# Two-layer hybrid encoder: FFN tiles placed anew, inputs normalised by halves, residual spilled by half rows

## The chip, the cores and the metric

One NeuronCore of one Trainium2 chip runs the whole program. The metric is the device time of one execution in microseconds. The kernel before took 2791.24 us as the median of three runs (2791.16, 2791.24 and 2794.4).

The engines are called PE (matrix products), DVE (VectorE), ACT (ScalarE), POOL (GpSimd) and SP (SyncE, which only issues DMAs here). Each works through its own queue in order. The queues' order is not the program's: a planner in the compiler puts each engine's instructions in order beforehand, by times that it estimates itself.

## What is computed

Two encoder layers on 1024 tokens of width 1024, all in float32. Layer 0 mixes tokens with differential attention, layer 1 with windowed grouped-query attention. Each layer then has a gated FFN with a depthwise convolution over positions, and a gated projection of a second input `p`:

```python
for i in range(DEPTH):                       # DEPTH = 2
    hn = rms_norm(h, attn_norm[i])
    mix = diff_attention(hn, ...) if i == 0 else windowed_gqa(hn, ...)
    h = h + mix                              # mix ends in a product with w_o
    h = h + conv_ffn(rms_norm(h, ffn_norm[i]), ffn_w_up[i], ffn_conv_w[i], ffn_conv_b[i], ffn_w_down[i])
    gate = sigmoid(rms_norm(h, ple_norm[i]) @ ple_w_gate[i])
    h = h + (p[i] @ ple_w_proj[i]) * gate
return rms_norm(h, final_norm)

def conv_ffn(h, w_up, conv_w, conv_b, w_down):        # D_FF = 2816
    u = h @ w_up                                      # 1024 x 5632
    u = sum(pad(u)[:, t:t + S] * conv_w[t] for t in range(3)) + conv_b
    gate, val = split(u, 2)
    return (silu(gate) * val) @ w_down
```

## The kernel before, in words

Activations lie transposed: features on the 128 partitions, the 1024 positions along the free dimension, in two halves of 512 (`HS`, index `hf`). `res[kt]`, kt = 0 to 7, is the residual stream. To keep float32 precision with fast products, each operand is split into a high part (a cast on ACT, L132 `copy_hi`) and the rest (a subtraction on DVE or POOL, L138 `sub_lo`), and each product is made of three matmuls (L227 to L229 in `mm3`, L1084 to L1086 in `product`).

Per layer the stages follow one another: projection to q, k, v; attention; `projected` (L1378), which holds the out-projection `out_proj` (L936), `p_proj` (L1243), `seven_inputs` (L988) and `ffn_up` (L1088); then `ffn_down` (L1179) and the gated projection. Each stage takes its tiles from pools that are stacked upon each other in on-chip memory. When a stage ends its pools go, and the next stage's pools are stacked from the same base. A tile of the new stage waits until the old tiles that lay at its place are done with, tile by tile. Within one pool the tags lie in the order in which they are first used.

- `out_proj` makes units of one row block and one half, 24 matmuls each. A unit's sum is taken off PSUM by an addition of the old residual (L964), which a DMA has fetched from the spill (L962). `half_order` (L970) has the last blocks run half 0, then half 1, and calls `done(hf)`, which gives `rstd[hf]`, the scale of the norm, by `norm_half` (L482). Afterwards the new residual is spilled whole (`spill_res`, L556), since its place is needed.
- `p_proj` makes `p @ ple_w_proj` in 16 units of 6 matmuls and stores them (L1277, L1279).
- `seven_inputs` normalises all of `res` (L1004, into tiles `nh`) and forms from it the inputs of the up-projection. The up-projection runs by a scheme of seven products for a 2 x 2 block product: 22 blocks j, each with seven products m1 to m7 of 12 matmuls. The inputs are b11 (`q1`), b21 and b22 (`qb`), t1 and t2 (`qa`, in the memory of the residual) and t3 and t4 (`qu`), each in two parts. `seven_weights` (L1039) makes the sums of the weights (`sf`, on DVE for the first two blocks, on POOL for the others) and splits four tiles of them (L1057, L1058); three of the four stand in the ring of `wh`/`wl` tiles, two of each, which `out_proj` and `p_proj` use as well.
- Block 0 runs the seven products side by side, k by k (L1121 to L1138), so that it can begin with the first inputs. The others run them one after another (L1139 to L1157). m1 and m2 add up in bank `pa`, m5 and m3 in bank `pc`; between m5 and m3, DVE reads m5 (L1149). The convolution follows (L1159 to L1177), and the result goes to memory as `gs[j]`.
- `ffn_down` takes two `gs` tiles a group (`load`, L1188: DMA into `gr`, high part `gh`, rest `gl`), 11 groups of 96 matmuls in 16 units. In group 0 the sum of a unit is added to the old residual, which comes by DMA from the spill (L1212 to L1214); in the others to `res` (L1216).

`stage` (L1373) makes the pools of the first projection, of `projected`'s first part, and of everything from `ffn_down` to the projection of layer 1. Its small pool (`t`, `n`) lies at the base, then come 24 places of 4 KB, of which the lists at L91 to L97 (`S_LOW`, `S_MID`, `S_END`, `XO`) give out numbers. Eight of these, `S_END`, hold a half of the normalised input in the projections, and `gh` and `gl` in `ffn_down`.

## Time and profile before

| | us |
|---|---|
| median of 3 runs | 2791.24 |
| the profiled execution, whole | 2790.52 |
| its span, first to last instruction | 2788.7 |
| PE busy | 2644.0 |
| DVE busy | 1958.8 |
| ACT busy | 1210.2 |
| POOL busy | 1016.0 |

The rows further down come from the profiled execution; times in them count from the span's start. A row of a timeline gives start and duration, engine, source line, operation, what it writes and reads, and in brackets how long its engine had been idle before it and what ended that. A busy PE is not always a PE at its peak: matmuls overlap, and the clock that is granted to TensorE varies, so the windows give the mean granted clock (PEclk, 1.00 is 2.4 GHz, 0.50 is 1.2 GHz).

### The profile page before, as it was taken

What the parts mean: (1) busy time and instruction counts of PE and PEld (TensorE: products, weight loads), DVE (VectorE), ACT (ScalarE), POOL (GpSimd) and SP (SyncE); (2) the same over time, 40 slices, a digit from 0 to 9 for tenths busy, and PEclk for the clock granted to TensorE, in tenths of its full rate; (3) what the DMA queues carried; (4) which work ended last, traced back from release to release, by engine and by line L of the source; (5) the groups of instructions that cost most, each with busy time, mean ns of one, the idle gap of its engine ahead of it and who ended that gap; (6) DMA issues with size and microseconds to landing.
All of it is one profiled execution on the core that took longest, in us unless ns stands there. A gap on an engine that the chain in (4) does not pass through costs nothing. (4 is left out here: it accounts for less than half of the span.)

```text
span 2788.7 us, 33239 instructions
## 1 busy us (share of the span) xinstructions
PE 2644.0 (95%) x12606; PEld 2183.4 (78%) x12606; DVE 1958.8 (70%) x2314; ACT 1210.2 (43%) x2101; POOL 1016.0 (36%) x587
## 2 busy tenths in 40 slices
PE   8999899999899999979999999999799999799998
PEld 6888778878668888858888788887588888688877
DVE  7541588883498888856677756963798888666664
ACT  5322567772444444421136426963443444311152
POOL 2642577773013443422221354441034344222201
PEclk9999999999999999989999999999899999899999
DMA  6444423303322322253213346113222232443112
GB/s 225 167 152 150 136 61 107 106 5 106 132 64 81 91 72 87 91 175 112 91 46 127 135 162 227 46 61 130 82 87 72 91 91 68 157 132 104 61 61 98
DMA packets 201828, 296.23 MB, mean 106 GB/s; under 512 B 9268, under 2 KB 138437, under 8 KB 197957
## 3 DMA queue, kind: packets, MB, share of 16 engines
q1 hardware_dynamic: 201045, 293.72, 32.1%
q8 instruction: 99, 1.62, 0.3%
q14 instruction: 60, 0.49, 0.1%
q10 hardware_dynamic: 624, 0.39, 0.0%
HBM read 207.83 MB, written 86.25 MB: 105 GB/s over the span
## 5 line engine op out<-in xcount | busy, mean ns | idle before, releaser
L138 POOL TENSOR_TENSOR wl<-wr,wh 128x1024 fp32r<-128x1024 f32 (+1 forms) x113 | 293.1, 2609 | 817.6 <-ACT wh L132 743.9
L1048 POOL TENSOR_TENSOR sf<-wr 128x1024 f32<-128x1024 f32 x40 | 128.4, 3210 | 585.3 <-DVE w L1058 585.3
L1216 DVE TENSOR_TENSOR res<-res,ps 128x512 f32<-128x512 f32 x320 | 216.6, 684 | 140.4 <-PE ps L229 140.4
L227 PE MATMUL ps<-gh,wh 128*128 128x512 f32 x704 | 275.6, 397 | 34.9 <-ACT gh L132 32.3
L228 PE MATMUL ps<-gl,wh 128*128 128x512 f32 x704 | 275.5, 391 | 0.0
L229 PE MATMUL ps<-gh,wl 128*128 128x512 f32 x704 | 274.9, 391 | 0.0
L227 PE MATMUL ps<-hn,wh 128*128 128x512 f32 x544 | 214.7, 396 | 5.6 <-ACT wh L132 4.9
L228 PE MATMUL ps<-hn,wh 128*128 128x512 f32 x544 | 212.9, 392 | 0.0
L229 PE MATMUL ps<-hn,wl 128*128 128x512 f32 x544 | 212.4, 392 | 0.1
L132 ACT CAST wh<-wr 128x1024 fp32r<-128x1024 f32 (+1 forms) x140 | 144.9, 1091 | 121.5 <-PE ps L228 62.7
L132 ACT CAST gh<-gr 128x1024 fp32r<-128x1024 f32 x44 | 46.2, 1050 | 343.3 <-PE ps L229 328.9
L733 DVE TENSOR_REDUCE sm<-S 128x1 f32<-128x1024 f32 x128 | 152.0, 1215 | 56.0 <-PE S L732 54.9
L227 PEld LDWEIGHTS ps<-gh,wh 128*128 128x128 f32 x704 | 134.4, 191 | 66.3 <-ACT gh L132 34.1
L737 ACT ACTIVATE e<-S,sm 128x1024 f32<-128x1024 f32 x128 | 142.2, 1113 | 90.0 <-DVE sm L733 87.6
L1057 ACT CAST w<-sf 128x1024 fp32r<-128x1024 f32 x88 | 92.6, 1052 | 174.4 <-PE ps L1086 106.6
L228 PEld LDWEIGHTS ps<-gl,wh 128*128 128x128 f32 x704 | 133.3, 189 | 27.6
L229 PEld LDWEIGHTS ps<-gh,wl 128*128 128x128 f32 x704 | 133.0, 189 | 27.9
L749 POOL TENSOR_TENSOR e<-e,e 128x1024 f32<-128x1024 f32 x64 | 152.3, 2380 | 5.2
L1084 PE MATMUL ps<-qa,w 128*128 128x512 f32 x352 | 138.6, 397 | 10.5 <-ACT qa L1023 8.1
L1084 PE MATMUL ps<-qb,w 128*128 128x512 f32 x352 | 140.2, 398 | 6.0 <-DVE uv L1149 3.3
L1086 PE MATMUL ps<-qa,w 128*128 128x512 f32 x352 | 138.9, 395 | 2.6 <-DVE w L1058 2.6
L1085 PE MATMUL ps<-qa,w 128*128 128x512 f32 x352 | 139.3, 396 | 0.0
(259 smaller groups left out, 7210.3 us busy)
## 6 DMA issues: line engine op xcount, KB each, us to landing
wr<-ffn_w_up SPq DMA_DIRECT2D x88, 512.0 KB, 5.2
gs<-c SPq DMA_DIRECT2D x44, 512.0 KB, 2.9
wr<-ffn_w_down SPq DMA_DIRECT2D x22, 1024.0 KB, 5.0
gr<-gs SPq DMA_DIRECT2D x44, 512.0 KB, 3.7
spill<-res SPq DMA_DIRECT2D x32, 512.0 KB, 2.9
qs<-rhl SPq DMA_DIRECT2D x32, 512.0 KB, 3.1
old<-spill SPq DMA_DIRECT2D x64, 256.0 KB, 2.8
wr<-diff_w_qkv SPq DMA_DIRECT2D x12, 1024.0 KB, 5.9
```

The costliest lines, as they stand in the source:

```text
L132: self.nc.scalar.copy(out, in_)
L138: eng.tensor_tensor(out, in_, f32(hi), op=ALU.subtract)
L227: self.nc.tensor.matmul(out, ah, bh, start=first, stop=False)
L228: self.nc.tensor.matmul(out, ah, bl, start=False, stop=False)
L229: self.nc.tensor.matmul(out, al, bh, start=False, stop=last)
L733: v.tensor_reduce(sm[:, a : a + 1], ps[:], axis=AX.X, op=ALU.max, negate=True)
L737: nc.scalar.activation(e[:], ps[:], AF.Exp, bias=sm[:, a : a + 1], accum_out=sm[:, 2 + a : 3 + a])
L749: nc.gpsimd.tensor_tensor(ea[:], ea[:], eb[:], op=ALU.add)
L1084: mm(ps, ah, bh, start=first and i == 0, stop=False, skip_group_check=True)
L1085: mm(ps, ah, bl, start=False, stop=False, skip_group_check=True)
L1086: mm(ps, al, bh, start=False, stop=last and i == n - 1, skip_group_check=True)
L1216: v.tensor_tensor(self.res[dt][:, sl], self.res[dt][:, sl], acc[:], op=ALU.add)
```

## The change

- The residual's rows are paired (kt, kt + 4) in one tile instead of (2i, 2i + 1).
- `out_proj` spills each half row right after its addition, in 16 DMAs, to a new scratch tensor; `spill_res` is no longer called there. Its small pool has three `t` tiles instead of four.
- `seven_inputs` is split. `seven_begin` runs in `done(0)` and normalises half 0 of `res` in place, and makes b11 and b21. `seven_rest` runs after `p_proj` and makes the rest from half 1.
- The pools of both FFN stages are stacked anew. `qb` and `q1` lie at the base through all of `projected`; above them come first the tiles of `out_proj` (half 1, then half 0), later `qu`, `t`, `e`, `wd`, `sf`. `p_proj`'s output tiles are two of the places of half 0. In `stage` come `S_LOW` and four of `S_END`, then the small pool, then the other four of `S_END`, then `S_MID`, for all its users.
- The weight sums of block 1 are made on POOL.
- In the blocks after the first, m4 stands ahead of m5.
- In `ffn_down`, group 0 copies its sums into `res` on ACT; the old residual is added by POOL in groups 3 to 6, two whole rows in each.

```diff
     def rows_tile(self, rows, kt, name):
         if rows[kt] is None:
+            half = KT // 2
             t = self.resp.tile([P, 2, S], F32, tag="res", name=self.nm(name))
-            rows[kt // 2 * 2] = t[:, 0]
-            rows[kt // 2 * 2 + 1] = t[:, 1]
+            rows[kt % half] = t[:, 0]
+            rows[kt % half + half] = t[:, 1]
...
+        before = self.spill
+        self.spill = self.dram.tile([D, S], F32, name=self.nm("spill"))
...
-            nc.sync.dma_start(old, self.spill[dt * P : (dt + 1) * P, sl])
+            nc.sync.dma_start(old, before[dt * P : (dt + 1) * P, sl])
             self.rows_tile(self.res, dt, "res")
             nc.vector.tensor_tensor(self.res[dt][:, sl], pt[:], old, op=ALU.add)
+            nc.sync.dma_start(self.spill[dt * P : (dt + 1) * P, sl], self.res[dt][:, sl])
             self.norm_tile(st, dt, hf, self.res[dt][:, sl], t[:, 1])
-        self.half_order(w, blocks, unit, lambda hf: self.norm_half(st, hf, psum, END_BANKS))
+        def done(hf):
+            self.norm_half(st, hf, psum, END_BANKS)
+            if hf == 0:
+                self.seven_begin(layer, st["rstd"])
+
+        self.half_order(w, blocks, unit, done)
...
+    def normed(self, layer, kt, hf, rstd):
+        r = self.res[kt][:, hf * HS : (hf + 1) * HS]
+        self.nc.vector.scalar_tensor_tensor(
+            r, r, self.gcol("ffn", layer, kt), rstd[hf][:], op0=ALU.mult, op1=ALU.mult
+        )
+        return r
+
+    def two_parts(self, out, src, sign=None):
+        self.copy_hi(out[:, 0], src, sign)
+        self.sub_lo(self.nc.vector, out[:, 1], src, out[:, 0], sign)
+
+    def seven_begin(self, layer, rstd):
+        self.x7 = {n: [] for n in ("b11", "b21", "b22", "t1", "t2", "t3", "t4")}
+        for kp in range(KT // 2):
+            one = self.q1p.tile([P, 2, HS], F32R, "q1", self.nm("q1"))
+            self.two_parts(one, self.normed(layer, kp, 0, rstd))
+            self.x7["b11"].append((one[:, 0], one[:, 1]))
+            qb = self.qbp.tile([P, 2, 2, HS], F32R, "qb", self.nm("qb"))
+            self.two_parts(qb[:, :, 0], self.normed(layer, kp + KT // 2, 0, rstd))
+            for n, i in (("b21", 0), ("b22", 1)):
+                self.x7[n].append((qb[:, 0, i], qb[:, 1, i]))
+            self.x7["t1"].append(qb)
+
+    def seven_rest(self, layer, rstd, fp):
+        v = self.nc.vector
         sub = ALU.subtract
+        qbs, self.x7["t1"] = self.x7["t1"], []
         for kp in range(KT // 2):
+            n1 = self.res[kp]
+            n2 = self.res[kp + KT // 2]
+            b12 = self.normed(layer, kp, 1, rstd)
+            b22 = self.normed(layer, kp + KT // 2, 1, rstd)
             ta = fp.tile([P, 2, HS], F32, "t", self.nm("ta"))
             tb = fp.tile([P, 2, HS], F32, "t", self.nm("tb"))
+            v.tensor_tensor(ta[:, 0], b12, n1[:, :HS], op=sub)
+            v.tensor_tensor(ta[:, 1], b22, ta[:, 0], op=sub)
+            v.tensor_tensor(tb[:, 0], b12, b22, op=sub)
+            v.tensor_tensor(tb[:, 1], ta[:, 1], n2[:, :HS], op=sub)
+            self.two_parts(qbs[kp][:, :, 1], b22, -1.0)
             qa = self.resp.tile([P, 2, 2, HS], F32R, tag="res", name=self.nm("qa"))
             qu = fp.tile([P, 2, 2, HS], F32R, "qu", self.nm("qu"))
+            for q, t, names in ((qa, ta, ("t1", "t2")), (qu, tb, ("t3", "t4"))):
+                self.two_parts(q, t[:])
...
-            w = self.seven_weights(raw, fp, j < 2)
+            w = self.seven_weights(raw, fp, j < 1)
...
                 v.tensor_tensor(t3[:], t2[:], pd[:], op=ALU.add)
+                prod(pe, "m4")
+                v.tensor_tensor(uv[:, lo], t3[:], pe[:], op=ALU.subtract)
                 prod(pc, "m5")
                 v.tensor_tensor(uv[:, hi], t3[:], pc[:], op=ALU.add)
                 prod(pa, "m2", False)
                 nc.scalar.copy(ug[:, lo], pa[:])
-                prod(pe, "m4")
-                v.tensor_tensor(uv[:, lo], t3[:], pe[:], op=ALU.subtract)
                 prod(pc, "m3", False)
...
                 if g == 0:
                     self.rows_tile(self.res, dt, "res")
-                    old = tp.tile([P, HS], F32, tag="n", name=self.nm("old"))
-                    nc.sync.dma_start(old[:], self.spill[dt * P : (dt + 1) * P, sl])
-                    v.tensor_tensor(self.res[dt][:, sl], old[:], acc[:], op=ALU.add)
+                    nc.scalar.copy(self.res[dt][:, sl], acc[:])
...
+            if g in (3, 4, 5, 6):
+                for dt in (2 * g - 6, 2 * g - 5):
+                    old = tp.tile([P, S], F32, tag="t", name=self.nm("old"))
+                    nc.sync.dma_start(old[:], self.spill[dt * P : (dt + 1) * P, :])
+                    nc.gpsimd.tensor_tensor(self.res[dt], self.res[dt], old[:], op=ALU.add)
...
-    def stage(self, ctx, name, places=range(24)):
+    def stage(self, ctx, name):
+        hp = Bank(ctx, self.tc, f"h_{name}", S_LOW + [S_END[i] for i in (0, 4, 1, 5)])
         tp = self.slots(ctx, f"t_{name}", {"t": 4, "n": 2})
-        hp = Bank(ctx, self.tc, f"h_{name}", list(places))
+        rest = Bank(ctx, self.tc, f"i_{name}", [S_END[i] for i in (2, 6, 3, 7)] + S_MID)
+        hp.pools.update(rest.pools)
         return tp, hp
...
+        with ExitStack() as c0:
+            self.qbp = self.slots(c0, f"qb{layer}", {"qb": 4})
+            self.q1p = self.slots(c0, f"q1{layer}", {"q1": 4})
+            with ExitStack() as c:
+                hp = Bank(c, self.tc, f"h_w{layer}", XO[1] + XO[0])
+                tp = self.slots(c, f"t_w{layer}", {"t": 3, "n": 2})
+                psum = self.banks(c, f"w{layer}")
+                rstd = self.out_proj(w, hp, tp, psum, "ffn", layer)
+                for _ in self.p_proj(
+                    layer, out_pp, psum, BANKS,
+                    lambda n: hp.cycle(XO[0][5:7], [P, S], F32, n),
+                ):
+                    pass
+            with ExitStack() as c:
+                qu = self.slots(c, f"qu{layer}", {"qu": 4})
+                fp = self.slots(c, f"ft{layer}", {"t": 5})
+                fe = self.slots(c, f"fe{layer}", {"e": 4})
+                fw = self.slots(c, f"fw{layer}", {"wd": 2})
+                fs = self.slots(c, f"fs{layer}", {"sf": 1})
+                fp = Tags([qu, fp, fe, fw, fs])
+                psum = self.slots(c, f"pu{layer}", {"ps": 8}, PSUM)
+                x7 = self.seven_rest(layer, rstd, fp)
+                self.ffn_up(layer, x7, fp, psum, gs)
```

## Rows read from the trace of the kernel before

**Rows 1.** The page's busy line: us (share of the span) and instructions of each engine.

```profile
PE 2644.0 (95%) x12606; PEld 2183.4 (78%) x12606; DVE 1958.8 (70%) x2314; ACT 1210.2 (43%) x2101; POOL 1016.0 (36%) x587
```

**Rows 2.** Waits of PE: waiting line, releaser, us in total, times, longest.

```profile
PE ps L227 <- ACT gh L132: 32.3, 2, 16.2
PE ps L1084 <- ACT q L1011: 13.7, 5, 5.7
...
PE ps L1086 <- DVE w L1058: 2.6, 2, 1.3
```

**Rows 3.** Windows: length; busy PE, PEld, DVE, ACT, POOL; PEclk; DMA share; GB/s.

```profile
1217.86:1266.69 48.83, 46.85 (x192) 37.30 (x193) 28.52 (x37) 7.51 (x8) 4.77 (x2) 0.96 0.55 192
2431.15:2478.46 47.31, 46.92 (x192) 38.11 (x193) 27.76 (x37) 7.51 (x8) 5.75 (x2) 0.94 0.57 198
...
754.89:803.90 49.01, 37.86 (x113) 24.48 (x114) 48.29 (x66) 21.50 (x27) 0.00 (x0) 0.76 0.15 43
1017.70:1036.74 19.04, 19.04 (x85) 15.77 (x84) 16.67 (x15) 7.96 (x9) 7.82 (x4) 1.00 0.28 83
714.90:735.10 20.20, 19.01 (x88) 14.88 (x87) 9.99 (x14) 9.67 (x14) 5.18 (x2) 1.00 0.60 191
735.10:749.10 14.00, 14.00 (x63) 11.36 (x61) 0.00 (x0) 8.05 (x16) 0.00 (x0) 1.00 0.67 267
```

**Rows 4.** Timeline where `p_proj` ends: its last matmul on PE; DVE's next operation.

```profile
748.83 0.39 PE L229 MATMUL ps<-wh,wl 128*128 128x512 f32 x1
...
750.15 1.22 DVE L1058 TENSOR_TENSOR w<-wr,w 128x1024 fp32r<-128x1024 f32 x1 [15.13 <-ACT w L1057]
```

**Rows 5.** Groups by line, 750 to 803.9 (ACT: from 735): count, busy us, mean ns.

```profile
L1004 DVE SCALAR_TENSOR_TENSOR nh<-res,par,rstd 128x512 f32<-128x512 f32 x16 | 11.0, 742 | 2.1 <-DMA pp<-pp 2.1
...
L1024 DVE TENSOR_TENSOR qu<-tb,qu 128x1024 fp32r<-128x1024 f32 x4 | 4.9, 1215 | 0.0
...
L1015 DVE TENSOR_TENSOR ta<-nh 128x512 f32<-128x512 f32 x4 | 2.7, 680 | 0.0
...
L1277 ACT COPY pp<-ps 128x512 f32<-128x512 f32 x16 | 8.7, 602 | 7.5 <-PE ps L229 7.5
```

**Rows 6.** Timeline of PE at the end of `ffn_up` in layer 0.

```profile
1194.28 0.39 PE L1086 MATMUL ps<-qu,w 128*128 128x512 f32 x1
...
1198.58 0.50 PE L1084 MATMUL ps<-qb,w 128*128 128x512 f32 x1 [1.65 <-DVE uv L1149]
...
1217.86 1.65 PE L227 MATMUL ps<-gh,wh 128*128 128x512 f32 x3 [16.22 <-ACT gh L132]
```

**Rows 7.** SP's queue at the same place.

```profile
1208.45 0.37 SPq L159 DMA_DIRECT2D wr<-ffn_w_down  x1
1211.94 0.34 SPq L1177 DMA_DIRECT2D gs<-c  x1
1212.37 2.91 SPq L1190 DMA_DIRECT2D gr<-gs  x4
```

**Rows 8.** DMA issues: count, KB each, median us from issue to landing.

```profile
old<-spill SPq DMA_DIRECT2D x64, 256.0 KB, 2.8
```

**Rows 9.** Timeline of POOL and DVE; then a line's durations, min/median/max ns.

```profile
1017.18 3.33 POOL L1048 TENSOR_TENSOR sf<-wr 128x1024 f32<-128x1024 f32 x1 [11.07 <-DVE w L1058]
...
1018.28 3.30 DVE L1170 SCALAR_TENSOR_TENSOR c<-ug,conv,c 128x1023 f32<-128x1023 f32 x1
...
L1216 DVE TENSOR_TENSOR res<-res,ps x320: 667/686/689, 1250.1 to 2692.1; 128x512 f32<-128x512 f32 x160
```

**Rows 10.** Timelines of PE and SP at the attention's start; landing of a load.

```profile
251.50 0.39 PE L731 MATMUL S<-stk,stk 128*128 128x512 f32 x1
...
295.67 0.32 SPq L609 DMA_DIRECT2D stk<-ks  x1
...
311.72 0.55 PE L769 MATMUL ps<-v,aT 128*128 128x128 f32 x1 [1.79 <-DMA v<-vs]
...
stk<-ks SPq DMA_DIRECT2D x8, 1024.0 KB, 5.0
```

More of the change, by code (lines that the diff above doesn't have):

```diff
@@ L66, in tile, with __init__ @@
         return self.pool.tile(shape, dtype, tag=tag, bufs=self.bufs[tag], name=name)
+class Tags:
+    def __init__(self, slots):
+        self.of = {tag: s for s in slots for tag in s.bufs}
+    def tile(self, shape, dtype, tag, name):
+        return self.of[tag].tile(shape, dtype, tag, name)
 class Bank:
@@ L1037, in seven_inputs @@
-        return out
+            for q, t, names in ((qa, ta, ("t1", "t2")), (qu, tb, ("t3", "t4"))):
+                self.two_parts(q, t[:])
+                for i, n in enumerate(names):
+                    self.x7[n].append((q[:, 0, i], q[:, 1, i]))
+        return self.x7
     def seven_weights(self, raw, fp, hurry):
@@ L1381, in projected @@
         gs = [self.dram.tile([P, S], F32, name=self.nm("gs")) for _ in range(FT)]
-        with ExitStack() as c:
-            tp, hp = self.stage(c, f"w{layer}", XO[0] + XO[1])
-            psum = self.banks(c, f"w{layer}")
-            rstd = self.out_proj(w, hp, tp, psum, "ffn", layer)
-            self.spill_res()
-            for _ in self.p_proj(
-                layer, out_pp, psum, BANKS,
-                lambda n: tp.tile([P, S], F32, tag="t", name=n),
-            ):
-                pass
@@ L1392, in projected @@
-        with ExitStack() as c:
-            fp = self.slots(
-                c, f"u{layer}",
-                {"q1": 4, "qb": 4, "qu": 4, "sf": 1, "wd": 2, "t": 5, "e": 4},
-            )
-            psum = self.slots(c, f"pu{layer}", {"ps": 8}, PSUM)
-            x7 = self.seven_inputs(layer, rstd, fp)
-            self.ffn_up(layer, x7, fp, psum, gs)
+        with ExitStack() as c0:
[21 more added lines that the diff above has]
+                self.ffn_up(layer, x7, fp, psum, gs)
@@ L1469, in run @@
             self.swa(ap, psum, [])
-        gs = self.projected(1, io["swa_w_o"][0], pp[1], "ple")
+        gs = self.projected(1, io["swa_w_o"][0], pp[1])
         with ExitStack() as sc:
```

43 lines of the change are left out of this document (2 added, 41 removed).

## The prediction

> **What bounds the kernel now.** I read four views in this order: the page's busy line, the list of what TensorE waited for, the windows around the places it names, and the instructions inside them. The page [rows 1] has TensorE (PE) busy 95% of 2788.7 us, so what can be won is its idle time, and its time at half clock. The waits [rows 2] name two places, each passed once in each of the two layers: 32.3 us for two waits for a cast of `gh`, the entry to `ffn_down`, and 13.7 us for casts of `q`, the entry to `ffn_up`. In mid-stage nothing is to be had: a block of 84 matmuls keeps PE busy for 19.04 of 19.04 us [rows 3], and 96, a group of `ffn_down`, take 19.04 x 96 / 84 = 21.76.
>
> Up stage, layer 0: the last matmul before it ends at 749.2 [rows 4], its own last one at 1217.86 - 16.22 = 1201.6 [rows 6]. That is 452.4 us for 22 blocks, which at 19.04 are 418.9: 33.5 us too many. Of these, 1.65 is a wait ahead of the last product [rows 6] and 1.3 a wait in the third block [rows 2]; the other 30.5 lie in the first. In the window of the first block DVE is busy 48.3 of 49.0 us, and PE 37.9, at a mean granted clock of 0.76 (part at 2.4, part at 1.2 GHz) [rows 3]. So that block is bound by DVE, which makes all inputs of the stage there, while in the 14 us before it, 735.1 to 749.1, DVE does nothing at all [rows 3]. The scale `rstd` of half 1 was ready by 735 (750.15 less 15.13 idle [rows 4]); but the tiles `nh` lie over the output tiles of `p_proj`, and the weights' ring is held by it.
>
> Down stage: PE starts 16.2 us after it ended, on the cast of `gr` [rows 6]. SP issues the load of `gr` at 1212.37, right behind the store of the last `gs` at 1211.94 [rows 7]. Its data was long there; its memory was that of the conv tiles. Then the first two groups take 48.8 us and in layer 1 47.3 [rows 3], instead of 43.5: 5.3 and 3.8 too many. All in all 2 x (30.5 + 1.65 + 16.2) + 9.1 = 106 us.
>
> **Part by part.**
> *First half early (`seven_begin`).* 16 DVE operations, 8 of 0.74 and 8 of 0.68 us [rows 5], 11.4 by their durations, move to behind the `rstd` of half 0. From 714.9 to 735.1 DVE is busy 10.0 of 20.2 us [rows 3]: it becomes just full, and the subtractions that `p_proj` waits for and the `rstd` of half 1 can slip. 0 to 3 us, I take 1.5.
> *Second half (`seven_rest`).* 4 x (2 x 0.74 + 5 x 0.68 + 2 x 1.215) = 29 us of DVE by durations [rows 5]. It can start at 735: `qu`, `ta` and `tb` lie where the out-projection's inputs were, which are free by then, not where `p_proj` writes. 14 us go into the idle stretch, 15 remain. They meet the splits of the first weights, 3 x 1.22 + 0.68 = 4.3 us, which can't move: their ring slots are held to the last matmul of `p_proj`, and the first of them runs at 750.15 [rows 4]. So DVE is done about 750.2 + 19.3 = 769.5, and PE, from the first cast on, at 750.1 + 19.04 = 769.2. The two ends meet, so some of the waits stay. The sums of the second block move from DVE to POOL (`j < 1`): 1.22 + 2 x 0.68 = 2.6 us less for DVE, but POOL's sums of a block take 7.8 us [rows 3], at the same time. A DVE operation that met them took 3.30 us [rows 9], where 1024 columns take 1.22 otherwise: 2 us each for one or two. With the 1.5 from above I take the first block's end at 774 instead of 749.2 + 19.04 + 30.5 = 798.7. So 6 of the 30.5 stay; bounds 3, and 15 if ACT is the later one, which has the casts of the same tiles to make among 8.7 us of `p_proj`'s copies [rows 5]. Gain 2 x 24.5 = 49.
> The Trainium skill, page "SBUF — State Buffer", section "SBUF: two separate sides", says that a DVE operation with two SBUF inputs and a GpSimd operation that reads SBUF exclude each other for a whole instruction. The 3.30 agrees. By that rule in full DVE would lose all 7.8 us of POOL's sums, 3 us a layer more than I take: 2718 instead of 2712. It gives POOL's new additions no hold on DVE's `res` additions, which read PSUM: these stay within 667 and 689 ns in all 320 cases [rows 9].
> *Half-row spills.* 16 stores of 256 KB replace 8 of 512 KB, the same bytes. In SP's queue each waits for its DVE addition, and the next load of `old` stands behind it. That load lands in 2.8 us [rows 8], a unit of 24 matmuls lasts 5.4: nothing; without that slack it would be 3 us a unit. `old` has three buffers instead of four, `p_proj`'s output two instead of four: two copies of 0.6 [rows 5] and a landing, taken as 2.8, are 4 us a tile, 2 us a row block with two tiles, under the 2.7 that PE needs: nothing.
> *Entry to `ffn_down`.* `gr` now lies over `qu`, the first `gh` and `gl` over `q1`. In the tail the last `qu` matmul starts at 1194.28 [rows 6], 24 matmuls or 5.4 us of products before the end. From its issue at 1212.37 [rows 7] to the first product at 1217.86 the load and its cast took 5.5 us. If SP puts the load ahead of the last store, the gap is 0 to 3 us; behind the store before it, somewhat more. I leave 3 of the 17.85 us (bounds 0 and 8), and expect the clock to stay up. Gain 2 x 14.85 = 29.7.
> *No `old` in the first group.* ACT copies 16 x 0.6 us [rows 5] into `res` within 21.76 us; 8.1 of the 9.1 go. The old rows are added on POOL in groups 3 to 6, two in each, at most 3.3 us each, as the sum of the same width [rows 9]; POOL is busy 5.8 of 47 us in two groups [rows 3]. DVE's next addition to such a row stands behind it, but half a group (10 us) lies between, and eight PSUM banks let PE run on: nothing; if both fail, up to 6 us in each of eight groups.
> *New order of products.* `m4` before `m5`: in the tail this frees `qu` earlier. In mid-stage it costs nothing as long as `m3` finds its bank read (rival C).
> *The other stages move too.* `stage` serves the projections as well. Counting tiles in order, q and k of layer 0's first head lay over places 12 to 15, which are free before the v part, so a first unit of scores runs at 251.50, inside it [rows 10]. Now they lie over places 10, 11, 22 and 23, which hold the half of the normalised input that PE reads until 297. The trace shows what that does: the loads that lie over places 20 to 23 go out from 295.67 on, and 1 MB takes 5.0 us to land [rows 10]. So the first scores come at about 303 or later. Before, the values had to wait until 311.72 for `v` in any case [rows 10]. Price 0 to 14, I take 6: two for the moved unit, four of idling. In layer 1 the same loads wait only for the middle of the v part, but exp tiles lie over v's output buffers: 0 to 7, I take 1.5.
>
> **Sum.** 49 + 29.7 + 8.1 - 6 - 1.5 = 79.3. From the span 2788.7 that is 2709.4; outside the span lie 1.8 us (2790.5), and the median of the runs is 0.7 above that: 2712.
>
> **Rivals.** A, the entry to `ffn_up` stays bound by DVE or ACT: the early half pushes the second `rstd` back, the sums on POOL hold DVE, the first block starts in pieces and half clock returns. For it: 48.3 of 49.0 us busy. Against: 14 idle us in front. Half of the 49 stays away: 2736. B, the load of `gr` stays behind the last store: its memory changed, not its queue. For it: 0.4 us between the two issues. Against: a load of `w_down` did go out ahead of that store, at 1208.45 [rows 7]. The 29.7 and half of the 8.1 are lost: 2746. C, slower: `m3` adds onto the bank of `m5`, which DVE must first have read; only `m2` (2.7 us) is left between, where `m4` stood too. The 1.65 us of the tail are just this wait. For it: DVE is busy 16.7 of 19.04 us in a block [rows 3], with one operation of 3.30. From 79 / 42 = 1.9 us in each of the 42 blocks on, all the gain is gone; at 3.3 it is 139 us: 2851. Against it: no idle PE in a block now.
>
> **How the numbers follow.** Forecast 0.66, A 0.13, B 0.10, C 0.06, better than my lower end 0.05. Lower end: 3 instead of 6 left twice, no gaps, no price in the attention: 6 + 6 + 7.5 less, 2692. Upper end: A, and about B: 2744. A measurement tells 0.2%, 5.6 us, from no change. Faster takes in all but C, 0.93; C near its break-even gives same 0.02, slower 0.05.
>
> **What would show it.** The first block's end near 774, `seven_begin` on DVE between 715 and 735 and no idle DVE before 749; granted clock 1.0 at both entries; `gr` issued before the last `gs` store, and a gap under 4 us; no `old` before group 3; blocks still 19.04 and groups 21.76 us. Against me: a wait of `m3` for L1149's reading in every block, first scores after 310, DVE waiting for POOL's `res` with PE behind it.

## The result

The kernel after takes 2753.07 us (median of four runs, 2751.71 to 2755.4), the kernel before 2791.2 beside it: a ratio of 0.9862, 95% interval 0.9845 to 0.9879. It is faster by 38 us. The forecast was 2712 with a range of 2692 to 2744: the sign was right, the size was half of what was forecast, and the time lies outside the range. The profiled execution took 2753.88 us, its span is 2752.1, against 2788.7 before.

The page's busy line after, which answers to [rows 1] (us, share of the span, instructions of each engine):

```profile
PE 2633.3 (96%) x12606; PEld 2184.3 (79%) x12606; DVE 1947.6 (71%) x2276; ACT 1226.2 (45%) x2133; POOL 1076.2 (39%) x609
```

What PE waited for, against [rows 2] (waiting line, releaser, us in total, times, longest):

```profile
PE ps L237 <- DVE res L977: 12.2, 4, 5.5
PE ps L1107 <- ACT pp L1303: 9.9, 2, 5.0
...
PE S L881 <- ACT e L894: 8.5, 5, 5.3
PE S L742 <- DMA stk<-ks: 7.4, 1, 7.4
PE S L881 <- issue: 6.4, 1, 6.4
...
PE ps L237 <- DVE ug L1178: 4.0, 2, 2.1
PE ps L1107 <- DVE uv L1174: 3.3, 2, 1.7
```

The 32.3 us for casts of `gh` are gone, and so are the 13.7 for casts of `q`. But five waits stand high that were small or not there before: the sum of the out-projection (L977) ahead of `p_proj`, the copies of `p_proj` at the start of the first block, a load of `stk` at the start of layer 0's attention (S L742), and two at the start of layer 1's attention (S L881).

Where the 36.6 us that the span lost come from is read off the starts of PE's matmuls: each stretch runs from the start of one stage's last matmul to the start of the next one's, in both traces.

| stretch | forecast gain | layer 0: before, after | layer 1: before, after | gain |
|---|---|---|---|---|
| first projection | - | 296.61, 294.91 | - | 1.7 |
| v part to end of out-projection | -6 and -1.5 | 425.75, 424.81 | 242.17, 261.00 | 0.9 and -18.8 |
| `p_proj` | with the next line | 26.47, 36.45 | 27.11, 38.04 | -20.9 |
| end of `p_proj` to end of up stage | 49 | 452.42, 433.27 | 452.32, 433.05 | 38.4 |
| gap ahead of `ffn_down` | 29.7 | 16.61, 2.50 | 16.49, 2.29 | 28.3 |
| `ffn_down` | 8.1 | 257.80, 253.51 | 260.32, 257.10 | 7.5 |
| the rest | 0 | | | -0.5 |

So 42.7 us are missing from the 79.3, in two places: the entry to the up stage, with `p_proj`, gave 17.5 instead of 49, and layer 1's attention lost 18.8 instead of 1.5. Layer 0's start gave 2.6 where 6 were to be lost.

**`p_proj`.** All engines at its start, layer 0 (start, duration; in brackets the idle time before, and what ended it):

```profile
721.78 0.68 DVE L977 TENSOR_TENSOR res<-ps,old 128x512 f32<-128x512 f32 x1
722.26 5.10 POOL L148 TENSOR_TENSOR wl<-wr,wh 128x1024 fp32r<-128x1024 f32 x2 [40.39 <-ACT wh L142]
722.38 2.78 DVE L148 TENSOR_TENSOR q<-res,q 128x512 fp32r<-128x512 f32 x1
...
725.09 2.82 DVE L148 TENSOR_TENSOR qb<-res,qb 128x512 fp32r<-128x512 f32 x1
727.83 0.68 DVE L977 TENSOR_TENSOR res<-ps,old 128x512 f32<-128x512 f32 x1
...
728.56 0.80 PE L237 MATMUL ps<-wh,wh 128*128 128x512 f32 x1 [5.48 <-DVE res L977]
```

PE ended the out-projection at 719.73, but DVE's last sum of it (the L977 at 727.83) stands in the queue behind all 16 operations of `seven_begin`, and the last two subtractions of these run beside POOL and take four times their 0.69 us. So the sum comes at 727.83; PE, which wants its bank, stands still and then runs at half clock. The norm of half 1, which needs that sum, follows late:

```profile
746.88 0.69 DVE L479 SCALAR_TENSOR_TENSOR rstd<-nv,rstd 128x512 f32<-128x512 f32 x1
747.61 5.39 DVE L1010 SCALAR_TENSOR_TENSOR res<-res,par,rstd 128x512 f32<-128x512 f32 x8
```

Its `rstd` was there by 735 before the change [rows 4]. So the 14 idle us of [rows 3] weren't filled by `seven_rest`; between 735 and 749 DVE is still busy only 4.2 us, the first row here. The others are the stretch of half clock, the stretch from `seven_rest`'s start on, in which DVE is busy all the time (38.47 of 38.49 us), and a block in mid-stage, still 19.04 (columns as in [rows 3]):

```profile
735.00:749.00 14.00, 14.00 (x62) 11.24 (x61) 4.16 (x7) 7.40 (x11) 0.00 (x0) 1.00 0.19 75
728.50:734.00 5.50, 5.44 (x13) 4.09 (x13) 4.20 (x8) 0.63 (x1) 0.00 (x0) 0.50 0.77 224
747.61:786.10 38.49, 30.13 (x116) 22.81 (x115) 38.47 (x45) 19.07 (x27) 7.63 (x3) 0.91 0.42 146
1000.00:1019.04 19.04, 19.04 (x85) 15.77 (x85) 16.66 (x15) 7.97 (x10) 7.82 (x3) 1.00 0.28 83
```

**Layer 1's attention.** All engines from the end of the v part on:

```profile
1663.10 0.28 PE L239 MATMUL ps<-wh,hn 128*128 128x256 f32 x1
...
1665.35 0.32 SPq L652 DMA_DIRECT2D vs<-vhl  x1
...
1669.77 0.55 PE L881 MATMUL S<-k,q 128*128 128x256 f32 x1 [6.39 <-issue]
...
1671.43 0.69 DVE L889 TENSOR_REDUCE sm<-S 128x2 f32<-128x514 f32 x1 [2.50 <-PE S L886]
...
1676.88 0.48 ACT L894 ACTIVATE e<-S,sm 128x257 f32<-128x257 f32 x1 [10.01 <-DMA vs<-vhl]
...
1677.96 0.69 PE L881 MATMUL S<-k,q 128*128 128x384 f32 x1 [5.29 <-ACT e L894]
```

The first scores come 6.7 us after the v part, and the first exp waits for the store of v's last output (`vhl`), over whose buffer its tile lies, though the maximum it needs was there at 1672.1. Before, the first scores came 0.1 us behind the v part. The profile names no releaser for the first wait. But the loads of `q`, 2 MB each, leave late: in the kernel before 14.5 and 11.2 us ahead of the v part's last matmul, and they took 11.4 us to land; in the kernel after 7.6 and 7.2 us ahead of it. SP's queue before, then after:

```profile
1678.55 0.44 SPq L609 DMA_DIRECT2D q<-qs  x1
...
1681.86 0.32 SPq L609 DMA_DIRECT2D q<-qs  x1
```

```profile
1655.51 0.80 SPq L620 DMA_DIRECT2D q<-qs  x2
```

**The entry to `ffn_down`**, as forecast; SP's queue in layer 0, against [rows 7]:

```profile
1181.85 0.41 SPq L1213 DMA_DIRECT2D gr<-gs  x1
1184.88 0.34 SPq L1200 DMA_DIRECT2D gs<-c  x1
1185.27 15.89 SPq L1213 DMA_DIRECT2D gr<-gs  x6
...
1204.45 0.32 SPq L1200 DMA_DIRECT2D gs<-c  x1
```

The store at 1184.88 is that of the last block but one, the last store is the one at 1204.45. So the first load of `gr` goes out 22.6 us ahead of the last store; before, it stood right behind it. What is left of the gap isn't the load: PE's wait of 2.1 us there is for a sum that DVE takes off PSUM (ug L1178, in the list above).

### The profile page after: what moved, and what is told of

Its sections match the earlier page's. It is cut to its first block, busy times and chain, and to the rows that moved or that the text cites. A ratio compares the mean times of both kernels' runs of the same rounds, so it can differ in the third digit from the quotient of the medians.

```text
span 2752.1 us, 33264 instructions
## 1 busy us (share of the span) xinstructions
PE 2633.3 (96%) x12606; PEld 2184.3 (79%) x12606; DVE 1947.6 (71%) x2276; ACT 1226.2 (45%) x2133; POOL 1076.2 (39%) x609
## 5 line engine op out<-in xcount | busy, mean ns | idle before, releaser
L1071 POOL TENSOR_TENSOR sf<-wr 128x1024 f32<-128x1024 f32 x42 | 136.2, 3244 | 549.9 <-DVE w L1081 549.9
L238 PEld LDWEIGHTS ps<-gl,wh 128*128 128x128 f32 x704 | 132.5, 188 | 27.1
L1107 PE MATMUL ps<-qb,w 128*128 128x512 f32 x352 | 138.7, 394 | 13.2 <-ACT pp L1303 9.9
L1109 PE MATMUL ps<-qa,w 128*128 128x512 f32 x352 | 138.0, 392 | 2.9 <-DVE w L1081 2.9
L1108 PE MATMUL ps<-qb,w 128*128 128x512 f32 x352 | 137.8, 392 | 0.0
L1108 PE MATMUL ps<-qa,w 128*128 128x512 f32 x352 | 137.7, 391 | 0.1
```

The lines of the kernel that those rows point to most:

```text
L238: self.nc.tensor.matmul(out, ah, bl, start=False, stop=False)
L1107: mm(ps, ah, bh, start=first and i == 0, stop=False, skip_group_check=True)
L1108: mm(ps, ah, bl, start=False, stop=False, skip_group_check=True)
L1109: mm(ps, al, bh, start=False, stop=last and i == n - 1, skip_group_check=True)
```

## The experiments

Each starts from the kernel after, unless it says otherwise. "Up end" is the start of the up stage's last matmul, counted from that of the out-projection; the two numbers are the layers. The time is the median of four runs where an interval stands, else of one run. The four runs of one kernel lie up to 7 us apart, so single times tell little, and the stretches decide. These scatter too: in the kernels that share the part in question with the kernel after, layer 1's attention takes 259.2 to 261.0 us, its `p_proj` 35.7 to 38.1, and its up end comes at 468.3 to 471.3 (layer 0: `p_proj` 36.1 to 36.7, up end 469.4 to 470.0).

| kernel | attention, layer 1 | `p_proj` | up end | gap at `ffn_down` | time, us | ratio to before |
|---|---|---|---|---|---|---|
| before | 242.2 | 26.5, 27.1 | 478.9, 479.4 | 16.6, 16.5 | 2791.2 | 1 |
| after | 261.0 | 36.5, 38.0 | 469.7, 471.1 | 2.5, 2.3 | 2753.07 | 0.9845 to 0.9879 |
| e1_attn_places | 252.3 | 36.7, 36.4 | 470.0, 468.9 | 2.5, 2.3 | 2743.94 | 0.9806 to 0.9836 |
| e2_begin_after_rstd1 | 259.2 | 26.5, 27.1 | 467.7, 467.6 | 2.3, 2.4 | 2744.96 | 0.9813 to 0.9842 |
| e3_begin_after_p | 259.5 | 26.5, 28.6 | 461.9, 462.4 | 2.4, 2.3 | 2738.85 | 0.9785 to 0.9817 |
| e4_gr_at_base | 259.8 | 36.7, 35.7 | 469.9, 468.3 | 2.5, 4.6 | 2754.25 | |
| e5_old_stage_m0 | 244.0 | 36.7, 36.5 | 470.0, 469.1 | 4.6, 2.5 | 2741.28 | |
| e6_gr_over_conv | 259.4 | 36.6, 37.5 | 470.0, 470.0 | 2.2, 18.3 | 2771.54 | |
| e7_sums_on_dve | 259.5 | 26.5, 28.8 | 461.5, 461.8 | 2.4, 2.4 | 2736.37 | |
| e8_places_and_begin | 253.1 | 26.5, 27.1 | 461.9, 461.9 | 2.4, 2.5 | 2731.68 | 0.9771 to 0.9804 |
| e9_old_stage_and_begin | 245.8 | 26.5, 27.1 | 459.8, 461.4 | 4.6, 2.4 | 2721.86 | 0.9728 to 0.9763 |
| e10_new_places | 248.1 | 26.5, 27.1 | 459.8, 460.0 | 2.6, 2.3 | 2721.82 | 0.9726 to 0.9762 |
| e11_no_low_qu | 259.4 | 26.5, 28.7 | 457.5, 458.1 | 2.7, 2.3 | 2726.21 | |
| e12_m5_before_m4 | 259.4 | 36.6, 38.1 | 469.9, 471.3 | 0.2, 0.2 | 2756.03 | |
| e13_pool_off_p | 260.5 | 33.8, 34.5 | 467.1, 467.8 | 2.5, 2.3 | 2749.04 | |
| e14_old_stage_p0 | 260.6 | 36.1, 38.1 | 469.4, 471.3 | 2.3, 2.3 | 2755.78 | |

### Is it the early half that slows `p_proj`?

e2: `seven_begin` can't start before the scale of half 1.

```diff
-            if hf == 0:
+            if hf == 1:
+                self.glate = self.cp.tile([P, 8], F32, name=self.nm("glate"))
+                o = 16 + layer * 8
+                nc.vector.scalar_tensor_tensor(
+                    self.glate[:], st["rstd"][1][:, 0:8], 0.0, self.par[:, o : o + 8],
+                    op0=ALU.mult, op1=ALU.add,
+                )
                 self.seven_begin(layer, st["rstd"])
...
+        g = self.gcol("ffn", layer, kt) if hf else self.glate[:, kt : kt + 1]
         self.nc.vector.scalar_tensor_tensor(
-            r, r, self.gcol("ffn", layer, kt), rstd[hf][:], op0=ALU.mult, op1=ALU.mult
+            r, r, g, rstd[hf][:], op0=ALU.mult, op1=ALU.mult
```

> One edit to the changed kernel: the 16 DVE operations of seven_begin read a copy of the norm's weights that is made from the scale of half 1, so they can't run before that scale; all else stays. This takes the early half away. Theory (the early half pushes out-projection's last sum, and with it p_proj and the second scale, back): from the last matmul of the out-projection to the last of p_proj 36.4 and 38.0 us fall to 26 to 28; the second scale is ready near 735 instead of 747.6; but DVE then has all 53 us of the inputs to make from 735, so the first block ends about where it does now, near 790 in layer 0. Time 2745 to 2757. Rival (p_proj is slowed by its two output tiles, not by DVE's order): the stretch stays above 33 us, and the time goes up by 10 or more, as DVE's 11 us move behind the scale.

e3: the same, but in `p_proj`, behind its first loop, with

```diff
+            self.glate[:], f32(plv[:, 1, HS : HS + 8]), 0.0, self.par[:, o : o + 8],
```

> One edit to the changed kernel: the 16 DVE operations of seven_begin read a copy of the norm's weights that is made from the last low part of p, so they run behind the last sum of the out-projection and the four subtractions that p_proj waits for, but before the scale of half 1 where that is late. Theory (only the order on DVE was wrong, not the early half as such): p_proj's stretch 26 to 29 us as without the early half; the second scale ready at 735 to 738; the first block ends 8 to 11 us earlier in each layer than in the changed kernel. Time 2731 to 2740. Rival (DVE is full anyway, or p_proj's output tiles are the limit): p_proj's stretch falls, but the first block ends within 3 us of where it ends now, as ACT's copies and the weights' splits are the late ones; time 2747 to 2754.

Both bring `p_proj` back to 26.5 us in layer 0, and to 27.1 (e2) and 28.6 (e3) in layer 1, nearly the stretch of before. So the order in DVE's queue was the cause, not the two output tiles. In e2 the up stage ends 2.0 and 3.5 us earlier than in the kernel after (in layer 1 part of that can be scatter), with no early half at all; it did better than the "about where it does now" of its expectation: where the planner put it, the early half cost more than it gave. In e3, behind the work that PE waits for, it is worth 5.8 and 5.2 us a layer over e2, and 14 us over the kernel after (medians). DVE in e3:

```profile
721.08 0.69 DVE L977 TENSOR_TENSOR res<-ps,old 128x512 f32<-128x512 f32 x1 [1.69 <-PE ps L239]
...
726.05 1.87 DVE L148 TENSOR_TENSOR wl<-ps,wh 128x512 fp32r<-128x512 f32 x3
...
728.63 5.40 DVE L1009 SCALAR_TENSOR_TENSOR res<-res,glate,rstd 128x512 f32<-128x512 f32 x8
...
740.68 5.39 DVE L1009 SCALAR_TENSOR_TENSOR res<-res,par,rstd 128x512 f32<-128x512 f32 x8
745.99 1.22 DVE L1070 TENSOR_TENSOR sf<-wr 128x1024 f32<-128x1024 f32 x1
...
762.51 3.42 DVE L148 TENSOR_TENSOR qa<-ta,qa 128x1024 fp32r<-128x1024 f32 x1
765.85 2.31 DVE L148 TENSOR_TENSOR qu<-tb,qu 128x1024 fp32r<-128x1024 f32 x1
```

The last sum comes 0.4 us behind the start of its last matmul, the second half starts at 740.68 instead of 747.61, the up stage ends 7.8 and 8.7 us earlier than in the kernel after, and between 747.15 and 790 DVE is busy 41.2 of 42.9 us.

e13: the low parts of `p_proj`'s weights on DVE instead of POOL.

```diff
-        if self.hurry and i % 2 == 1:
+        if getattr(self, "all_dve", False) or self.hurry and i % 2 == 1:
             return self.nc.vector
...
+        self.all_dve = True
         wh, wl = self.wrows(self.io["ple_w_proj"][layer], 0, 2, 0, D)
+        self.all_dve = False
```

> One edit to the changed kernel: the low parts of p_proj's weights are subtracted on DVE instead of POOL; seven_begin stays where it is. DVE's queue keeps the last sum of the out-projection behind all 16 operations of seven_begin. Theory (of the 10 us that p_proj lost, some 4.2 are the two subtractions of 2.78 and 2.82 us that ran beside POOL's 5.10 us, the rest is the order in the queue): these two go back to 0.69, the last sum comes at about 723.6 instead of 727.8, PE's gap of 5.95 us ahead of p_proj shrinks to 1.5 to 2.5, and p_proj's stretch is 31 to 34 us instead of 36.4 and 38.0; 2.4 us of subtractions are added behind it on DVE. Rival (the order alone; POOL's part is no cause): the gap stays above 5 us and the stretch above 35.

```profile
722.22 0.68 DVE L148 TENSOR_TENSOR q<-res,q 128x512 fp32r<-128x512 f32 x1
722.82 0.69 DVE L148 TENSOR_TENSOR qb<-res,qb 128x512 fp32r<-128x512 f32 x1
723.42 0.69 DVE L977 TENSOR_TENSOR res<-ps,old 128x512 f32<-128x512 f32 x1
```

The two subtractions are back to 0.69, the sum comes at 723.42, PE's gap shrinks from 5.95 to 1.71 us, and `p_proj` by 2.7 and 3.6 us. So some 3 of the 10 us were POOL's hold, and the rest was the order, as e2 and e3 give all of it back in layer 0. The Trainium skill, page "SBUF — State Buffer", section "SBUF: two separate sides", says that a DVE operation with two SBUF inputs and a GpSimd operation that reads SBUF shut each other out for a whole instruction; the 2.78 and 2.82 beside POOL and the 0.68 and 0.69 without it agree.

### What limits the first block then?

e7 (from e3): the sums of block 1 on DVE.

```diff
-            w = self.seven_weights(raw, fp, j < 1)
+            w = self.seven_weights(raw, fp, j < 2)
```

> The kernel with seven_begin behind p (e3_begin_after_p) and one more edit: the weight sums of block 1 are made on DVE again, as before the change. Theory (POOL's sums hold DVE while the first block waits for DVE): the operations of 3.42, 2.31 and 1.77 us behind 762 go back to 1.22, 1.22 and 0.69, which is 4.4 us less, for 2.6 us of sums more: last up matmul of each layer 1 to 3 us earlier, counted from the out-projection's last. Rival (the sums themselves cost DVE as much as the hold did): within 1 us, or later by up to 3.

The held operations went back to 1.22 and 0.69 us, so the hold is real. The up end comes 0.4 and 0.7 us earlier, as the rival says. But e9 and e10 below have the same edit, and what else they change lies behind this stretch in layer 0; their up end there is 459.8, 2.1 us earlier than in e3, as the theory says (layer 1: 1.0 and 2.4). In layer 0 of e7 PE waits 1.9 us less than in e3, but its granted clock in the 45 us behind `p_proj` was 0.89, and 0.92 in e3, e9 and e10. So the edit is worth 0.4 to 2.4 us a layer, and theory against rival stays open.

e11 (from e3): no low parts of `qu`. The kernel leaves their share out of the products, so it is no substitute, and only its times are read.

```diff
+                lo = 1 if q is qa else 0
...
-                    self.x7[n].append((q[:, 0, i], q[:, 1, i]))
+                    self.x7[n].append((q[:, 0, i], q[:, lo, i]))
```

> The kernel with seven_begin behind p (e3_begin_after_p), and the low parts of qu (t3 and t4) are left out in both layers: its high parts are read in their place, the matmuls are as many as before. That takes four DVE subtractions a layer away, 1.21, 1.21, 1.22 and one of 2.31 us beside POOL, all in the first block. Theory (the first block is bound by DVE): from the out-projection's last matmul to the up stage's last 4 to 6.5 us less than the 461.9 and 462.4 of e3 in each layer, time 2726 to 2732. Rival (ACT's casts or the weights' tiles are the limit): under 2 us a layer.

Four subtractions of 6.0 us less on DVE, and the up stage ends 4.4 and 4.3 us earlier. DVE is what bounds the first block, in e3 as in the kernel before.

e8: e1 and e3 together, and eight places for `p_proj`'s output instead of two.

```diff
-                    lambda n: hp.cycle(XO[0][5:7], [P, S], F32, n),
+                    lambda n: hp.cycle([XO[0][i] for i in (0, 1, 2, 7, 3, 4, 5, 6)], [P, S], F32, n),
```

> Three edits to the changed kernel together: the pools of layer 1's attention in the order v, k1, q1, a, e, k0, q0 (as e1), seven_begin behind p (as e3), and eight places instead of two for p_proj's output. If they add up: 9 us from the first, 14 from the second, and from the third 0 to 6 us: with DVE as the limit of the first block nothing, with p_proj's copies as a second limit (ahead of block 0 PE waits 3.4 and 4.2 us in e3) 2 to 3 us a layer. Time 2724 to 2731; the second theory at its low end, the first at its high end. If the copies don't matter the wait ahead of block 0 stays as long as in e3.

The up end is that of e3 (461.9 in layer 0), within 0.5 us. In the kernel after, a wait of 5.0 us at the start of the first block is put down to copies of `pp`, but DVE has no idle time there either (the row from 747.61 on), and in e8, with more places for the copies, PE's longest wait there is again 5.0 us, now for DVE's `w`. Of the 23.3 us that e1 and e3 gave apart, 21.4 are there (2731.68).

### Is it the place of the tiles that slows layer 1's attention?

e1: only the order in which its pools are stacked.

```diff
+        if len(stacks) == 4:
+            names = ["v", "k1", "q1", "a", "e", "k0", "q0"]
+        else:
+            names = ["v", "a", "e"] + stacks
-        ap = Bank(ctx, self.tc, name, ["v", "a", "e"] + stacks)
+        ap = Bank(ctx, self.tc, name, names)
```

> One edit to the changed kernel: the pools of layer 1's attention are stacked v, k1, q1, a, e, k0, q0 instead of v, a, e, k0, q0, k1, q1. So the exp tiles no longer lie over the output buffers of the v part, and the first k and q lie over places that nothing uses since the q part. Theory (the place of the tiles): the stretch from the last matmul of the v part to the last of the out-projection, 261.0 us in the changed kernel and 242.2 before, comes back to 243 to 248; the waits 'S L881 <- issue' (6.4) and 'S L881 <- ACT e L894' (longest 5.3) are gone; time 2735 to 2741. Rival (the loads of q themselves, 2 MB each, are the limit, or the planner's order): one gap of over 4 us stays at the start, stretch 255 or more, time above 2746.

e5: the stage from `ffn_down` to the projection stacked as before the change.

```diff
+        if name == "m0":
+            tp = self.slots(ctx, f"t_{name}", {"t": 4, "n": 2})
+            return tp, Bank(ctx, self.tc, f"h_{name}", list(range(24)))
```

> One edit to the changed kernel: for the stages from layer 0's ffn_down to layer 1's projection alone, the pools are stacked as in the kernel before (small pool at the base, then the 24 places in order). Theory (all that layer 1's attention lost comes from where its tiles lie): the stretch from the last matmul of the v part to the last of the out-projection in layer 1 goes from 261.0 back to 241 to 245 us, although everything else of the change stays; in layer 0 the gap ahead of ffn_down goes from 2.5 to about 4.6, as it did in layer 1 when gr lay at the base there. Time 2735 to 2741. Rival (a part of the loss is the planner's new order or another part of the change): the stretch stays above 250.

e1 got back 8.7 of the 18.8 us and lies between its theory and its rival: its first scores still came 3.2 us late, on the load of q. e5 got back 17.0. The windows of this stretch, in order those of before, of after and of e5 (columns as in [rows 3]):

```profile
1693.06:1935.23 242.17, 234.08 (x1301) 199.69 (x1299) 173.23 (x291) 164.94 (x432) 95.08 (x142) 1.00 0.28 94
```

```profile
1663.10:1924.10 261.00, 240.41 (x1301) 203.64 (x1299) 177.19 (x299) 170.13 (x439) 95.14 (x142) 0.97 0.27 95
```

```profile
1669.24:1913.19 243.95, 234.27 (x1300) 201.06 (x1299) 177.00 (x299) 169.89 (x439) 94.97 (x142) 0.99 0.28 94
```

PE's idle time is 8.1, 20.6 and 9.7 us, and its busy time for the same matmuls 234.1, 240.4 and 234.3: of the 18.8 us, 12.5 were idling and 6.3 the lower clock that went with it (mean 0.97 instead of 1.00). The place of the tiles is the cause of some 17 us; the last 1.8 are no more than the scatter of this stretch.

### What holds the load of `gr`?

e4 and e6 move the small pool of the last stage alone, in layer 1: in e4 to the base, over `qb`; in e6 80 KB up, over the tiles of the convolution. e4, then e6:

```diff
+        if name == "m1":
+            tp = self.slots(ctx, f"t_{name}", {"t": 4, "n": 2})
...
-        tp = self.slots(ctx, f"t_{name}", {"t": 4, "n": 2})
+        if name != "m1":
+            tp = self.slots(ctx, f"t_{name}", {"t": 4, "n": 2})
```

```diff
+        if name == "m1":
+            low = S_LOW + [S_END[i] for i in (0, 4, 1, 5, 2, 6, 3, 7)] + S_MID[:4]
+            hp = Bank(ctx, self.tc, f"h_{name}", low)
+            tp = self.slots(ctx, f"t_{name}", {"t": 4, "n": 2})
+            hp.pools.update(Bank(ctx, self.tc, f"i_{name}", S_MID[4:]).pools)
+            return tp, hp
```

> One edit to the changed kernel, in the last stage alone (ffn_down and the gated projection of layer 1): the small pool with gr lies at the base again, over qb tiles, which the last two products of the up stage read; S_LOW and S_END follow. The order of the stores and loads in the program is the same. Theory (the entry to ffn_down was held by the place of gr): the gap between the last up matmul and the first down matmul of layer 1 goes from 2.3 back to 12 to 17 us, while that of layer 0 stays 2.5. Rival (the load went out earlier because the queue's order changed, or because half-row tiles changed it): layer 1 stays at 2 to 4 us.

> One edit to the changed kernel, in the last stage of layer 1 alone: the small pool with gr lies 80 KB above the base, over the t tiles that the convolution of the last blocks writes and the last gs store reads, as it did in the kernel before; the order of the program is the same. Theory (the load of gr waits for whatever lay at its place; with qb there it was 4.55 us, with the conv tiles it is the wait of the kernel before): the gap between the last up matmul and the first down matmul of layer 1 is 13 to 17 us, layer 0 stays at 2.5; time 2763 to 2770. Rival (the change of place doesn't matter, it was the new order of products or the earlier end of the blocks' work that let the load go): the gap stays at 2 to 5 us.

e4's theory had the number wrong (4.6 us, not 12 to 17), e6's had it nearly right (18.3). What counts is not "at the base" but who used the place last. SP's queue in e4, then in e6, with the last `gs` store at the end of the one and at the start of the other:

```profile
2387.39 0.34 SPq L1200 DMA_DIRECT2D gs<-c  x1
2390.34 10.31 SPq L1213 DMA_DIRECT2D gr<-gs  x5
...
2404.93 0.32 SPq L1200 DMA_DIRECT2D gs<-c  x1
```

```profile
2405.01 0.34 SPq L1200 DMA_DIRECT2D gs<-c  x1
2408.01 7.50 SPq L1213 DMA_DIRECT2D gr<-gs  x6
```

The last up matmul starts at 2392.0 in e4 and at 2394.3 in e6. Over `qb` the load leaves while m3 still runs, 14.6 us ahead of the last store, over the conv tiles 3.0 us behind it. No order in the program differs: the place does it.

e12: m5 ahead of m4 again, m4 between m2 and m3.

```diff
-                prod(pe, "m4")
-                v.tensor_tensor(uv[:, lo], t3[:], pe[:], op=ALU.subtract)
                 prod(pc, "m5")
...
                 nc.scalar.copy(ug[:, lo], pa[:])
+                prod(pe, "m4")
+                v.tensor_tensor(uv[:, lo], t3[:], pe[:], op=ALU.subtract)
                 prod(pc, "m3", False)
```

> One edit to the changed kernel: in the blocks after the first, m5 stands ahead of m4 again, and m4 between m2 and m3. Theory (the order only lets qu, and with it the place of gr, go some 5.4 us earlier at the end of the stage): gaps ahead of ffn_down 3 to 6 us instead of 2.5 and 2.3, blocks unchanged at 19.04; time 2753 to 2760. Rival (the order also costs or gains in each block, as m3 must wait for the reading of m5): the up stage changes by more than 3 us a layer.

The gap is 0.2 us, below what was expected, but the first group of `ffn_down` then takes 26.6 and 26.0 us instead of 22.8 and 22.7: in layer 0 PE waits 2.7 us inside it for `gh`, and its granted clock is 0.73 from 1193.6 to 1200. Gap and group together are 1.6 and 1.1 us longer than in the kernel after. In the blocks the order costs and gains nothing (up end within 0.3 us).

### What did layer 0's attention lose?

e14: the first projection's stage stacked as before the change, by e5's edit with

```diff
+        if name == "p0":
```

> One edit to the changed kernel: the pools of the first projection alone are stacked as in the kernel before (small pool at the base, 24 places in order). Theory (the late first scores of layer 0 cost next to nothing, since the time before was lost again to waits right behind): a first unit of scores runs inside the v part again, and the stretch from the last matmul of the v part to the last of the out-projection changes by less than 2 us from 424.8; time 2750 to 2755. Rival (they cost the 6 us of the forecast, and something else in the change gave them back): the stretch is 5 us or more shorter, 419 or less, time 2746 or less.

The out-projection ends at 719.86, in the kernel after at 719.73: no difference. The v part ends 2.9 us later, since a unit of scores runs inside it, and the rest is 2.8 us shorter (under 2 was expected, a miss: the shift had not been thought of). In the 50 us behind the v part PE waits 7.3 us in e14 and 9.6 in the kernel after, for other things: casts of exp tiles and `v` in the one, the load of `stk` in the other. So the early unit brings forward its own matmuls, and nearly all of that is waited for again behind them.

### Both kernels beaten

e9: the edits of e5, e3 and e7. e10: those of e3 and e7, and new places (in `stage`, then in `attn_pools`):

```diff
+        if name != "p0":
+            hp = Bank(ctx, self.tc, f"h_{name}", S_LOW)
+            tp = self.slots(ctx, f"t_{name}", {"t": 4, "n": 2})
+            end = [S_END[i] for i in (0, 4, 1, 5, 2, 6, 3, 7)]
+            hp.pools.update(Bank(ctx, self.tc, f"i_{name}", end[:6] + S_MID + end[6:]).pools)
+            return tp, hp
...
+        if len(stacks) == 4:
+            names = ["v", "a", "k1", "e", "k0", "q0", "q1"]
```

> Three edits to the changed kernel: the old stacking of pools between layer 0's ffn_down and layer 1's attention (as e5), seven_begin behind p (as e3), the sums of block 1 on DVE (as e7). If the causes are separate, the sum is 17 us from the first less 2 for the entry to ffn_down of layer 0, 14 from the second, 1 from the third: time 2722 to 2728, stretches as in those runs (attention of layer 1 with its out-projection 241 to 245, p_proj 26 to 29). If the loss of the attention had to do with seven_begin's time as well, it doesn't add up, and the time is above 2731.

> Three edits to the changed kernel: seven_begin behind p, the sums of block 1 on DVE, and new places for the stages from layer 0's ffn_down on: S_LOW at the base, then the small pool (gr over q1), then six of S_END, S_MID, two of S_END; layer 1's attention stacked v, a, k1, e, k0, q0, q1. So exp tiles lie over the half of the normalised input that is free first, the first k and q over the same middle places as before the change, and nothing that is wanted early over v's output buffers. Theory (both losses and the gain at ffn_down are matters of place and can be had together): attention of layer 1 with its out-projection 241 to 246 us, gaps ahead of ffn_down 2 to 4 us in both layers, time 2720 to 2726. Rival (e1's 8 us that didn't come back were the planner's order): attention 249 or more, time above 2728.

They take 2721.9 and 2721.8 us, ratios of 0.9745 and 0.9744 to before, 31 us less than the kernel after. The causes add up. e10 has the short gap at `ffn_down` in both layers, but its attention keeps 6 us over that of before, which lies between its theory and its rival; why is open.

## Why the forecast was wrong, point by point

- **`seven_begin`, priced 0 to 3, taken 1.5; `p_proj` took 10.0 and 10.9 us longer.** The step that failed is the price put on "it becomes just full, and the subtractions that `p_proj` waits for and the `rstd` of half 1 can slip". The durations were right (about 0.67 us from one start to the next). But room in a stretch isn't a place in a queue: DVE works in the planner's order, which put the out-projection's last sum behind 16 operations that nobody wanted yet. e2 and e3 show the order, e13 the 3 us of POOL's hold, which the forecast looked for in the first block only.
- **`seven_rest`, "it can start at 735".** It started at 747.61, since the second `rstd` needs that sum; of the 14 idle us, 9.8 stayed idle. This was rival A, "the early half pushes the second `rstd` back", and "half clock returns" (0.50 from 728.5 to 734), given 0.13 and priced at half of the 49. It took 31.5 of them: 8.5 and 9.4 us in `p_proj` over the 1.5 allowed, and the rest, about 7 us a layer, in the first block. That block ended at about 788 (the last up matmul at 1189.45, less 21 blocks of 19.04 and 1.65), 68.2 us behind the out-projection, where the forecast had 774 - 722.4 = 51.6.
- **DVE's work in the first block** was summed too low: next to `seven_rest` and 4.3 us of splits stand block 0's own sums (1.22 + 2 x 0.69), splits of block 1 and 4.4 us of hold by POOL. e3, with the second half begun at 740.68, still ends block 0 at 461.9 - 401.5 = 60.4 us behind the out-projection, not 51.6.
- **Sums on POOL, "2 us each for one or two".** Three operations were held, 4.4 us in all, about the upper end of what was allowed. As DVE would otherwise have had the sums, e7, e9 and e10 make this worth 0.4 to 2.4 us a layer. By the rule of the Trainium skill, page "SBUF — State Buffer", section "SBUF: two separate sides", told in full, the forecast gave 2718: the three operations agree with the rule, but the miss of 41 us lies elsewhere.
- **Layer 1's attention, priced 0 to 7, taken 1.5; it cost 18.8.** The mechanism was named ("exp tiles lie over v's output buffers") and mis-sized: a wait of 5 us for `vhl`'s store, and 6.3 us of lower clock that follow. The other step failed outright, "the same loads wait only for the middle of the v part": the loads of `q` left only 7.6 us ahead of its end, and the first scores came 6.7 us late. That it was these loads is argued for the kernel after, and shown in e1, where PE's wait of 2.9 us is for `q`. e5 shows the place of the tiles as the cause of nearly all of it.
- **Layer 0's attention, taken 6; nothing lost.** The first scores came at 302.7, as forecast ("at about 303"). But e14 shows that the price of the moved unit was counted without the waits behind it, which were there before in any case.
- **Entry to `ffn_down`, 29.7 forecast, 28.3 measured.** e4 and e6 show the mechanism. Rival B is wrong: the place held the load, the queue didn't. The size came out close, but what is left is not what was foreseen: the 1.65 us ahead of the last product are still there (1.7), and 2.1 of the gap's 2.5 us are a wait for DVE that the forecast didn't name.
- **Groups 0 and 1, 8.1 forecast, 7.1 measured (7.5 for the whole of `ffn_down`).** ACT's copies and POOL's additions in groups 3 to 6 cost next to nothing: group 0 takes 22.8 us, groups 1 to 9 21.76 each, and the last, into which products of the next stage are mixed, 34.9 and 38.5, where it took 34.9 and 38.9 before.
- **Half-row spills and two output tiles for `p_proj`, priced at nothing**: right for the spills (in e2 `p_proj` takes the time of before, and the second `rstd` comes 1.3 us later behind the out-projection), and for the tiles once the order is right: with eight of them (e8) layer 0's `p_proj` and up end are those of e3 within 0.1 us. That e3's `p_proj` in layer 1 is 1.5 us longer isn't the tiles: e9 and e10, with two of them, take 27.1 too, and e3's granted clock there was 0.94, theirs 1.00.
- **Rival C is wrong**: blocks stay at 19.04, and e12's old order doesn't change the up end.

## What to carry to other kernels

Work that is moved forward into idle time must also stand, in its engine's queue, behind what others wait for; where a planner sets the order, give the moved work a true dependence on the last urgent operation. When tiles get new places, list for each tile that is wanted early who used its place last, in every stage that shares the layout: the same edit gave 28 us at one boundary and lost 17 at another. After a removed wait, add up all the work of the engine that bounds the place, other users' included, from the time when its last input is there.

## What the runs showed of the hardware

- A DVE subtraction of two SBUF operands beside a POOL subtraction took 2.78 and 2.82 us instead of 0.69 (three 3.42, 2.31 and 1.77 instead of 1.22, 1.22 and 0.69 beside POOL's sums in e3), while three `wl<-ps`, with one input in PSUM, took 1.87 us together in e3 (from 726.05) with POOL in such a subtraction all the time.
- PE's clock at one boundary: behind the 2.50 us ahead of `ffn_down` the granted clock stayed at 1.00 (1191.9 to 1200) in the kernel after; in e3, where 2.40 us and then 1.03 us passed without a matmul's start, its mean was 0.60 from 1184.9 to 1190 (part at 1.2 GHz), and the first group took 25.7 us instead of 22.8.
